# A transformer block on one core: first norm with tokens on partitions, and the first stage's vector work regrouped

## The chip, the core and the metric

The kernel runs on one core of a Trainium2 chip. The metric is the device time of one execution in microseconds (us), lower is better. The core has five engines that run their own instruction streams: TensorE (PE, matrix products), VectorE (DVE), ScalarE (ACT), GpSimd (POOL) and SyncE (SP, which here issues every transfer). An engine takes its instructions in order and waits on semaphores for the others.

## The reference

One block with 256 tokens and 1024 features, all in float32. `c` makes six vectors of 1024 (shift, scale and gate of two halves), the normed input is scaled and shifted by them, one wide projection gives seven parts, and attention, a gating unit and a feed-forward follow:

```python
mod = silu(c) @ w_ada + b_ada                      # shift1, scale1, gate1, shift2, scale2, gate2
h = rmsnorm(x, g_mix) * (1 + scale1) + shift1
q, k, v, u, vs, ga, gb = split(h @ w_in)           # 512,512,512,512,512,1024,1024 columns
y_attn = causal_attention(q, k, v) @ w_proj_attn   # 8 heads of 64
y_sgu = spatial_gating(gelu(u), gelu(vs)) @ w_proj_sgu
x = x + gate1 * ((sigmoid(ga) * y_attn + sigmoid(gb) * y_sgu) @ w_out)
h = rmsnorm(x, g_ffn) * (1 + scale2) + shift2
x = x + gate2 * (square(relu(h @ w_ff1)) @ w_ff2)  # 4096 wide
return rmsnorm(x, g_final)
```

`rmsnorm` divides each token by the root of the mean of its squares (plus 1e-6).

## The kernel before

**Products.** A float32 product is made of three products in a faster 32-bit format. Every operand is split into a high part (ACT's cast `whi`, `hh`) and the rest (DVE's subtraction `wlo`, `hl`), and PE adds high·high, high·low and low·high in one accumulator. So each weight chunk of 128 x 2048 costs ACT a cast, DVE a subtraction and PE 48 or 36 products, and it arrives by a transfer of 1 MB into one of five `raw` buffers. Accumulators are banks of a pool of eight (`bank()`).

**Head.** SP loads a table of columns (`cols_sb`), x turned (`xT`, features on partitions) into `x_sb`, and the first chunks. ACT squares x, DVE adds the four squares, PE sums them over the partitions (`sums`), ACT and POOL make one over the root (`rstd`), and PE spreads it over all partitions (`spread`). POOL then multiplies seven of the eight feature tiles of x by it (`xn`, line 298), DVE the first. PE also runs small idle products (`spin`).

**First stage (lines 250 to 330).** A loop of eight turns, one for each tile `kt` of 128 features. A turn has two chunks: one of `w_ada` (columns of scale1 and shift1) and one of `w_in` (columns for q, k, v and vs). DVE makes two dot products of the ada chunk with silu(c) (`junk`, each with a sum `acc`), from them the columns `acol` and `bcol`; ACT makes `hh` = xn · acol + bcol, DVE the same in full precision (`hf`) and the difference `hl`; ACT and DVE split the `w_in` chunk; PE then runs 24 products of 256 columns and 12 of 512. In this stage the order of PE, DVE and ACT is that of the code (`InOrder`, pinned). I call the moment when PE starts the first product of turn k S(k).

**Middle and rest.** From `high(0)` on the order is not pinned: a scheduler lays out what each engine issues. In ten turns PE runs u, ga and gb (`wide(n)`) from streamed chunks while ACT, DVE and PE also do attention (pairs of heads: scores, exponentials, norm, transposes, products with v) and the gating unit. Then come the projections, `w_out`, the feed-forward in 16 units and the last norm. `x_sb` is read again as the residual at `w_out`.

Of the kernel before, what the change touches and what calls it, by code (L numbers as in the profile page):

```python
# [34 lines left out]
class InOrder:  # L35
    """An engine whose instructions are issued in the order in which they are traced."""
# [11 lines left out]
def block_kernel(ctx, tc, xT, cols, wsguT, bsgu, w_a1, w_1, w_a, w_m, w_f, out):  # L48
# [138 lines left out]

    # the middle's weight chunks, and the adaLN chunks that are used beside them
# [62 lines left out]
    hh = act.tile([P, KT, S], F32R, name="hh", tag="b1")  # L251
    hl = act.tile([P, KT, S], F32R, name="hl", tag="b2")
    rb1 = wk.tile([P, S], F32, name="rb1", tag="sqa", bufs=1)
    xn = act.tile([P, KT, S + 2], F32, name="xn", tag="b3")
    wsg = const.tile([P, 8, P], F32, name="wsg", tag="c4")
    bsg = const.tile([P, NP, P], F32, name="bsg")
    for kt in range(KT):
        if kt + 2 < KT:
            ada[kt + 2] = load(w_a1[kt + 2], 2 if kt + 2 == KT - 1 else 1)
            wraw[kt + 2] = load(w_1[kt + 2], 4 if kt + 2 == KT - 1 else 2)  # L260
        raw, w_raw = ada.pop(kt), wraw.pop(kt)
        np_ = 4 if kt in (0, KT - 1) else 2
        wh = his.tile([P, 2048], F32R, name="whi", tag="whi")
        wl = los.tile([P, 2048], F32R, name="wlo", tag="wlo")
        hf = wk.tile([P, S], F32, name="hf", tag="hf", bufs=2)
        wp = [slice(2048 // np_ * i, 2048 // np_ * (i + 1)) for i in range(np_)]

        def w_hi(i):
            ACT.copy(out=wh[:, wp[i]], in_=w_raw[:, wp[i]])

        def w_lo(i):
            DVE.tensor_tensor(out=wl[:, wp[i]], in0=w_raw[:, wp[i]], in1=wh[:, wp[i]].bitcast(F32), op=ALU.subtract)

        def cols_ab():
            column(da, SCALE1, kt)
            column(db, SHIFT1, kt)

        def h_hi():
            a, b = acol[:, 0, kt:kt + 1], bcol[:, 0, kt:kt + 1]
            ACT.activation(out=hh[:, kt], in_=xn[:, kt, 0:S], func=AF.Identity, scale=a, bias=b)  # L280
            DVE.tensor_scalar(out=hf, in0=xn[:, kt, 0:S], scalar1=a, scalar2=b, op0=ALU.mult, op1=ALU.add)

        def h_lo():
            DVE.tensor_tensor(out=hl[:, kt], in0=hf, in1=hh[:, kt].bitcast(F32), op=ALU.subtract)

        da, db = dot(raw, 0), dot(raw, 1)
        if kt == 0:
            for i in range(3):
                w_hi(i)
            cols_ab()  # L290
            rp = spread(rs1)
            spin(4)
            DVE.tensor_tensor(out=xn[:, 0, 0:S], in0=x_sb[:, 0], in1=rp[:, 0:S], op=ALU.mult)
            h_hi()
# [9 lines left out]
            qk_ps = [bank() for _ in range(4)]
            vv_ps = [[bank() for _ in range(2)] for _ in range(2)]
        else:
            w_hi(0)
            cols_ab()
            h_hi()
            w_lo(0)  # L310
            w_hi(1)
            h_lo()
            for i in range(1, np_):
                w_lo(i)
                if i + 1 < np_:
                    w_hi(i + 1)
        f, l = kt == 0, kt == KT - 1
        for ft in range(8):
            o = qk_ps[ft // 2][:, S * (ft % 2):S * (ft % 2) + S]
            w = slice(P * ft, P * ft + P)  # L320
            mm3(o, wh[:, w], wl[:, w], hh[:, kt], hl[:, kt], f and ft % 2 == 0, l,
                skip_group_check=ft % 2 == 1)
        for n in range(2):
            w = slice(1024 + 512 * n, 1536 + 512 * n)
            for t in range(2):
                tk = slice(P * t, P * t + P)
                o = vv_ps[n][t]
                PE.matmul(out=o, lhsT=hh[:, kt, tk], rhs=wh[:, w], start=f, stop=False)
                PE.matmul(out=o, lhsT=hl[:, kt, tk], rhs=wh[:, w], start=False, stop=False)
                PE.matmul(out=o, lhsT=hh[:, kt, tk], rhs=wl[:, w], start=False, stop=l)  # L330
# [134 lines left out]
    A0, S0, TD, OD = 1, 5, 2, 3  # when attention and the gating unit start; lags of transposes and products  # L465
    for n in range(10):
# [7 lines left out]
        if n == 0:  # L474
# [240 lines left out]
def _ko(w, cols):  # L715
    """[K, N] -> chunks [N/cols][128][K/128 * cols] with k in (ko, p)."""
# [42 lines left out]
```

## Time and profile before

| | us |
|---|---|
| median of 3 runs (lowest, highest) | 376.79 (376.47, 377.02) |
| span of the profiled execution, first to last instruction | 374.84 |
| around the span, to that median | 1.95 |
| PE busy | 358.4 (96%) |
| DVE busy | 266.4 (71%) |
| ACT busy | 206.0 (55%) |
| POOL busy | 15.4 (4%) |

The profiled execution's own time is known by its span; what lies around the span is taken from the median. Busy time is an average over stages, and PE's 96% hides where it waits. PE's waits as the profile lists them are 3.3 and 3.1 us in the head, 2.4 us for `hl`, 1.2 us for `hh` and 0.5 us for the root.

### The profile page before, as it was taken

Reading aid. Unit: us, or ns where it says so; the run is one execution under the profiler, and the core shown is the slowest. Engines: PE = TensorE matmul, PEld = TensorE weight load, DVE = VectorE, ACT = ScalarE, POOL = GpSimd, SP = SyncE. Lnnn points to the kernel's source line nnn. Section 1 sums busy time; section 2 is a strip of 40 time slices with the busy share of each in tenths; the row PEclk is TensorE's granted clock in tenths of the full one; section 3 lists DMA queues with packets and bytes.
Section 4 is the critical chain, followed back from the end, with each engine's and each line's share of the span. In section 5 each row is a group of like instructions: output and inputs, shape, how many; then the busy total and the mean of one; then the engine's idle time right before and its main releaser. Section 6 shows DMA issues by size and latency. Waiting matters only on the chain.

```text
span 374.8 us, 6928 instructions
## 1 busy us (share of the span) xinstructions
PE 358.4 (96%) x2884; PEld 346.5 (92%) x2884; DVE 266.4 (71%) x420; ACT 206.0 (55%) x283; POOL 15.4 (4%) x21
## 2 busy tenths in 40 slices
PE   4779999999999999999999999999999999999993
PEld 3469989999899999999999999999999999999993
DVE  2899997687989986899856755766656545546442
ACT  4424346999894374356566544655445645446242
POOL 1460000010000000000000000000000000000001
PEclk9999999999999999999999999999999999999997
DMA  7999999987789995467755494764856554500003
GB/s 246 410 348 346 346 348 398 320 321 259 269 309 357 353 396 226 152 232 282 251 210 189 150 334 147 299 231 150 299 202 257 217 201 147 215 1 2 2 0 112
DMA packets 16126, 89.34 MB, mean 238 GB/s; under 512 B 1888, under 2 KB 2400, under 8 KB 7136
## 3 DMA queue, kind: packets, MB, share of 16 engines
q1 hardware_dynamic: 16096, 88.92, 64.9%
q8 instruction: 22, 0.36, 0.4%
q14 instruction: 8, 0.07, 0.0%
HBM read 87.86 MB, written 1.05 MB: 237 GB/s over the span
## 4 chain that ended last, share of the span: by engine, by line
PE 92%; issue 3%; DVE 3%; POOL 1%; POOLq 0%; DVEq 0%; ACT 0%
PE bank L44 92%; DVE junk L44 1%; DVE wlo L44 1%; POOL rs L120 0%; DVE hl L44 0%; DVE ys L44 0%; POOLq L755 0%; DVEq L755 0%; DVE acol L44 0%; DVE xn L44 0%; POOL maskf L103 0%; DVE maskf L44 0%; DVE idle L44 0%; ACT ms L44 0%; DVE ones L44 0%
## 5 line engine op out<-in xcount | busy, mean ns | idle before, releaser
L44 ACT CAST whi<-raw 128x2048 fp32r<-128x2048 f32 (+2 forms) x74 | 112.6, 1537 | 79.3 <-PE bank L44 77.7
L44 DVE TENSOR_TENSOR wlo<-raw,whi 128x2048 fp32r<-128x2048 f32 (+2 forms) x74 | 135.8, 1842 | 9.1 <-ACT whi L44 7.9
L44 PE MATMUL bank<-zh,whi 128*128 128x258 f32 x256 | 72.5, 283 | 0.0
L44 PE MATMUL bank<-zh,wlo 128*128 128x258 f32 x256 | 72.3, 282 | 0.0
L44 PE MATMUL bank<-zl,whi 128*128 128x258 f32 x256 | 72.2, 282 | 0.0
L44 PE MATMUL bank<-fl,whi 128*128 128x256 f32 x256 | 72.0, 281 | 0.0
L44 PE MATMUL bank<-fh,wlo 128*128 128x256 f32 x256 | 71.9, 281 | 0.0
L44 PE MATMUL bank<-fh,whi 128*128 128x256 f32 x256 | 71.9, 281 | 0.0
L44 PE MATMUL bank<-hl,whi 128*128 128x256 f32 x224 | 63.5, 283 | 2.4 <-DVE hl L44 2.4
L44 PE MATMUL bank<-hh,whi 128*128 128x256 f32 x224 | 64.5, 288 | 1.2 <-ACT hh L44 1.2
L44 PE MATMUL bank<-hh,wlo 128*128 128x256 f32 x224 | 63.3, 282 | 0.0
L44 DVE SCALAR_TENSOR_TENSOR junk<-raw,csb 128x1024 bf16<-128x1024 f32 x48 | 58.4, 1239 | 0.0
L44 PEld LDWEIGHTS bank<-fh,whi 128*128 128x128 f32 x256 | 49.1, 192 | 0.0
L44 PEld LDWEIGHTS bank<-zl,whi 128*128 128x128 f32 x256 | 48.4, 189 | 0.0
L44 PEld LDWEIGHTS bank<-zh,whi 128*128 128x128 f32 x256 | 48.3, 189 | 0.0
L44 PEld LDWEIGHTS bank<-zh,wlo 128*128 128x128 f32 x256 | 48.3, 189 | 0.0
L44 PEld LDWEIGHTS bank<-fh,wlo 128*128 128x128 f32 x256 | 48.1, 188 | 0.0
L44 PEld LDWEIGHTS bank<-fl,whi 128*128 128x128 f32 x256 | 48.0, 188 | 0.0
L44 PEld LDWEIGHTS bank<-hh,whi 128*128 128x128 f32 x224 | 42.9, 192 | 3.2 <-ACT hh L44 2.0
L44 PEld LDWEIGHTS bank<-hl,whi 128*128 128x128 f32 x224 | 42.7, 191 | 3.3 <-DVE hl L44 2.9
L44 PEld LDWEIGHTS bank<-hh,wlo 128*128 128x128 f32 x224 | 42.8, 191 | 0.0
L44 DVE TENSOR_TENSOR fl<-r,fh 128x512 fp32r<-128x512 f32 x16 | 11.1, 694 | 30.2 <-PE bank L44 28.9
(132 smaller groups left out, 488.7 us busy)
## 6 DMA issues: line engine op xcount, KB each, us to landing
raw<-in_w_f SPq DMA_DIRECT2D x32, 1024.0 KB, 4.8
raw<-in_w_a SPq DMA_DIRECT2D x22, 1024.0 KB, 5.8
raw<-in_w_m SPq DMA_DIRECT2D x16, 1024.0 KB, 6.5
raw<-in_w SPq DMA_DIRECT2D x12, 512.0 KB, 6.6
raw<-in_w_a SPq DMA_DIRECT2D x4, 512.0 KB, 6.8
raw<-in_w SPq DMA_DIRECT2D x8, 256.0 KB, 7.2
x_sb<-in_xT SPq DMA_DIRECT2D x2, 512.0 KB, 5.2
raw<-in_w_m SPq DMA_DIRECT2D x4, 256.0 KB, 6.8
```

Of the source, the lines that this page charges most:

```text
L44: return lambda *a, **k: pin(op(*a, **k))
```

## The change

- x is loaded with tokens on partitions (`xt`, one half per transfer). ACT's square sums each token by itself (an added column holds the 1e-6), POOL makes one over the root per half, DVE scales the first half and ACT the second, and PE turns both with 16 transposes into four banks (`xps`). `xn` is copied from there by ACT (`keep`). POOL multiplies nothing; one POOL power is issued early on constants.
- `x_sb` is loaded from `xT` later, in the middle's sixth turn, for the residual alone. The gating unit's tables are loaded two turns later than before.
- In the first stage's turns after the first, ACT makes `acol`, `bcol` and `hf` too. DVE keeps the dots, `wlo` and `hl`.
- PE's products of a turn go pass by pass (all high·high, then high·low, then low·high) and not column tile by column tile. Their number is the same.
- Idle products: 8 and 6 in place of 4 and 4. The turned banks are allocated, and those of q, k, v and vs too, ahead of the loop.

```diff
-    for i in range(2):
-        nc.sync.dma_start(out=x_sb[:, 4 * i:4 * i + 4], in_=xT[:, 4 * i:4 * i + 4])
+    for t in range(2):
+        nc.sync.dma_start(out=xt[:, t, 0:D], in_=x[t])
+        DVE.memset(xt[:, t, D:D + 1], (EPS * D) ** 0.5)
...
+    rs1 = const.tile([P, 2], F32, name="rs1")
+    nc.gpsimd.tensor_tensor(out=rs1, in0=ones[:, 0:2], in1=nhalf, op=ALU.pow)
...
-    for i in range(4):
-        ACT.activation(out=sqs[i], in_=x_sb[:, 2 * i:2 * i + 2], func=AF.Square)
-        if i:
-            DVE.tensor_tensor(out=sqs[0], in0=sqs[0], in1=sqs[i], op=ALU.add)
...
-    spin(4)
-    rs1 = rstd(ss, D)
+    for t in range(2):
+        sq = act.tile([P, D + 1], F32, name="sq", tag=("b1", "b2")[t])
+        ACT.activation(out=sq, in_=xt[:, t], func=AF.Square, scale=D ** -0.5, accum_out=ms1[:, t:t + 1])
+        nc.gpsimd.tensor_tensor(out=rs1[:, t:t + 1], in0=ms1[:, t:t + 1], in1=nhalf[:, 0:1], op=ALU.pow)
+    DVE.tensor_scalar(out=xt[:, 0, 0:D], in0=xt[:, 0, 0:D], scalar1=rs1[:, 0:1], scalar2=None, op0=ALU.mult)
+    for w in (slice(0, P), slice(P, D)):
+        ACT.activation(out=xt[:, 1, w], in_=xt[:, 1, w], func=AF.Copy, scale=rs1[:, 1:2])
+    xps = [bank() for _ in range(4)]
+    for t in range(2):
+        for kt in range(KT):
+            at = S * (kt % 2) + P * t
+            PE.transpose(out=xps[kt // 2][:, at:at + P], in_=xt[:, t, P * kt:P * kt + P], identity=ident)
+    spin(6)
...
+            if n == 0:
+                ACT.activation(out=bcol[:, n, at], in_=acc, func=AF.Identity, bias=b)
+            else:
+                DVE.tensor_tensor(out=bcol[:, n, at], in0=acc, in1=b, op=ALU.add)
...
-            for i in range(1, KT):
-                nc.gpsimd.tensor_tensor(out=xn[:, i, 0:S], in0=x_sb[:, i], in1=rb1, op=ALU.mult)
...
+        column(db, SHIFT1, kt)
+        ACT.activation(out=hh[:, kt], in_=xk, func=AF.Identity, scale=a, bias=b)
+        if f:
+            DVE.tensor_scalar(out=hf, in0=xk, scalar1=a, scalar2=b, op0=ALU.mult, op1=ALU.add)
+        else:
+            ACT.activation(out=hf, in_=xk, func=AF.Identity, scale=a, bias=b)
             w_lo(0)
...
+        for fts in (range(0, 4), range(4, 8)) if np_ == 4 else (range(0, 8),):
+            for p, (w, h) in enumerate(((wh, hh), (wh, hl), (wl, hh))):
+                for ft in fts:
...
+        if n == 5:
+            nc.sync.dma_start(out=x_sb, in_=xT)
-        if n == 0:
+        if n == 2:
             nc.sync.dma_start(out=wsg, in_=wsguT)
```

Three places of the order in which the engines now issue. The first is DVE in one turn of the first stage, from the two dots of a turn to the dots of the next; before:

```order
L44 SCALAR_TENSOR_TENSOR junk,acc<-raw,csb 128x1024 x2
L44 SCALAR_TENSOR_TENSOR acol<-acc,cols_sb,pre 128x1
L44 TENSOR_TENSOR bcol<-acc,cols_sb 128x1
L44 TENSOR_SCALAR hf<-xn,acol,bcol 128x256
L44 TENSOR_TENSOR wlo<-raw,whi 128x1024
L44 TENSOR_TENSOR hl<-hf,hh 128x256
L44 TENSOR_TENSOR wlo<-raw,whi 128x1024
L44 SCALAR_TENSOR_TENSOR junk,acc<-raw,csb 128x1024 x2
```

The same turn on DVE now:

```order
L44 SCALAR_TENSOR_TENSOR junk,acc<-raw,csb 128x1024 x2
L44 TENSOR_TENSOR wlo<-raw,whi 128x1024
L44 TENSOR_TENSOR hl<-hf,hh 128x256
L44 TENSOR_TENSOR wlo<-raw,whi 128x1024
L44 SCALAR_TENSOR_TENSOR junk,acc<-raw,csb 128x1024 x2
```

Three instructions have left DVE's turn; the second `wlo` still stands ahead of the next turn's dots. The second place is ACT in a turn of the first stage, from the cast of a chunk's first half on; before:

```order
L44 CAST whi<-raw 128x1024
L44 ACTIVATE hh<-xn,bcol,acol 128x256
L44 CAST whi<-raw 128x1024 x2
L44 ACTIVATE hh<-xn,bcol,acol 128x256
L44 CAST whi<-raw 128x1024 x2
```

The same on ACT now (the pair of casts is the second half of this turn's chunk and the first half of the next one's):

```order
L44 CAST whi<-raw 128x1024
L44 ACTIVATE acol<-acc,pre,cols_sb 128x1
L44 ACTIVATE bcol<-acc,cols_sb 128x1
L44 ACTIVATE hh<-xn,bcol,acol 128x256
L44 ACTIVATE hf<-xn,bcol,acol 128x256
L44 CAST whi<-raw 128x1024 x2
```

`acol`, `bcol` and `hf` have come to ACT, and the cast of the second half stands behind them. The third place is ACT in the middle, where the second pair of heads is normed (`pr<-pr,rc`), the first pair's transposes are copied (`pt`) and the third pair's exponentials follow (`pr,sm<-bank,mx`, four pieces); before:

```order
L44 ACTIVATE pr<-pr,rc 128x128
L44 COPY pt<-bank 128x384
L44 CAST whi<-raw 128x2048
L44 COPY pt<-bank 128x384
L44 ACTIVATE pr,sm<-bank,mx 128x256
L44 ACTIVATE pr,sm<-bank,mx 128x128
L44 ACTIVATE pr,sm<-bank,mx 128x256
```

The same place now:

```order
L44 ACTIVATE ga_sb<-bank 128x2x256
L44 COPY pt<-bank 128x384 x2
L44 ACTIVATE pr<-pr,rc 128x256
L44 ACTIVATE pr<-pr,rc 128x128
L44 ACTIVATE pr<-pr,rc 128x256
L44 ACTIVATE pr<-pr,rc 128x128
L44 ACTIVATE pr,sm<-bank,mx 128x256
L44 CAST whi<-raw 128x2048
L44 ACTIVATE pr,sm<-bank,mx 128x128
```

A chunk's cast now stands between the first and the second piece of the third pair's exponentials. PE's own order from the first attention product on is the same as before.

## Rows read from the trace of the kernel before

**Rows 1.** Chain that ended last: start us, us, what.

```profile
26.07 341.85 PE bank L44 x2807
```

**Rows 2.** Timeline of PE, first stage: start us, us, operation, wait before.

```profile
24.55 0.38 PE L44 MATMUL bank<-hh,whi 128*128 128x256 f32 x1 [1.23 <-ACT hh L44]
...
28.02 0.41 PE L44 MATMUL bank<-hl,whi 128*128 128x256 f32 x1
28.23 0.41 PE L44 MATMUL bank<-hh,wlo 128*128 128x256 f32 x1
...
33.20 0.28 PE L44 MATMUL bank<-hh,whi 128*128 128x256 f32 x1
...
61.34 0.28 PE L44 MATMUL bank<-hh,whi 128*128 128x256 f32 x1
```

**Rows 3.** Busy by stretch: PE, PEld, DVE, ACT, POOL, granted clock, DMA share, GB/s.

```profile
28.00:29.00 1.00, 1.00 (x7) 1.00 (x6) 1.00 (x3) 0.00 (x0) 0.00 (x0) 0.50 0.83 209
```

**Rows 4.** Timeline of all engines, head and first turn.

```profile
6.10 2.44 ACT L44 ACTIVATE sq<-x_sb 128x512 f32<-128x512 f32 x4 [3.37 <-DMA x_sb<-in_xT]
...
10.96 1.87 PE L44 MATMUL bank<-idle 128*128 128x512 bf16 x4
...
11.48 1.75 POOL L120 TENSOR_TENSOR rs<-ms,nhalf 128x2 f32<-128x2 f32 x1 [9.39 <-ACT ms L44]
...
15.94 8.46 POOL L298 TENSOR_TENSOR xn<-x_sb,rb 128x256 f32<-128x256 f32 x7 [2.70 <-ACT rb L44]
...
19.70 1.76 DVE L44 SCALAR_TENSOR_TENSOR junk<-raw,csb 128x1024 bf16<-128x1024 f32 x1
```

**Rows 5.** Transfers: timeline of SP, and time to landing of the transfers issued from 6.0, 9.9.

```profile
6.09 0.33 SPq L66 DMA_DIRECT2D raw<-in_w_a  x1
7.38 1.61 SPq L66 DMA_DIRECT2D raw<-in_w  x2
9.94 0.33 SPq L66 DMA_DIRECT2D raw<-in_w_a  x1
...
raw<-in_w_a SPq DMA_DIRECT2D x1, 1024.0 KB, 10.0
...
raw<-in_w_a SPq DMA_DIRECT2D x1, 1024.0 KB, 11.2
```

**Rows 6.** Timeline of DVE and ACT in one turn of the first stage.

```profile
27.07 1.21 DVE L44 SCALAR_TENSOR_TENSOR junk<-raw,csb 128x1024 bf16<-128x1024 f32 x1
...
28.21 0.08 DVE L44 DVE_READ_ACCUMULATOR junk<-raw,csb 128x1 f32 x1
...
29.50 0.15 DVE L44 TENSOR_TENSOR bcol<-acc,cols_sb 128x1 f32<-128x1 f32 x1
29.74 0.60 ACT L44 ACTIVATE hh<-xn,bcol,acol 128x256 fp32r<-128x256 f32 x1 [3.36 <-DVE bcol L44]
...
30.24 1.98 ACT L44 CAST whi<-raw 128x1024 fp32r<-128x1024 f32 x2
...
31.55 1.22 DVE L44 TENSOR_TENSOR wlo<-raw,whi 128x1024 fp32r<-128x1024 f32 x1
32.69 1.22 DVE L44 SCALAR_TENSOR_TENSOR junk<-raw,csb 128x1024 bf16<-128x1024 f32 x1
```

**Rows 7.** Groups by form: busy us, mean ns, idle before and its releaser.

```profile
L44 ACT ACTIVATE ms<-bank,eps 128x2 f32<-128x2 f32 x3 | 0.8, 259 | 2.5 <-PE bank L44 2.5
...
L496 POOL TENSOR_TENSOR vrs<-vms,nhalf 128x2 f32<-128x2 f32 x1 | 0.7, 698 | 46.3 <-DVE vms L44 46.3
```

**Rows 8.** Middle: timeline of ACT and PE, and ACT's casts of the streamed chunks (group).

```profile
62.24 0.60 ACT L44 ACTIVATE qT<-bank 128x512 f32<-128x512 f32 x1 [1.73 <-PE bank L44]
...
92.65 0.40 ACT L44 ACTIVATE pr<-bank,mx 128x128 f32<-128x128 f32 x1
...
96.49 0.39 PE L44 MATMUL bank<-hh,whi 128*128 128x256 f32 x1
...
L44 ACT CAST whi<-raw 128x2048 fp32r<-128x2048 f32 x48 | 91.7, 1913 | 77.7 <-PE bank L44 77.7
```

More of the change, by code (lines that the diff above doesn't have):

```diff
@@ L47, in block_kernel @@
 @with_exitstack
-def block_kernel(ctx, tc, xT, cols, wsguT, bsgu, w_a1, w_1, w_a, w_m, w_f, out):
+def block_kernel(ctx, tc, x, xT, cols, wsguT, bsgu, w_a1, w_1, w_a, w_m, w_f, out):
     nc = tc.nc
@@ L76, in block_kernel @@
     nc.sync.dma_start(out=cols_sb, in_=cols)
+    xt = act.tile([P, 2, D + 1], F32, name="xt", tag="b4")
+    for t in range(2):
+        nc.sync.dma_start(out=xt[:, t, 0:D], in_=x[t])
+        DVE.memset(xt[:, t, D:D + 1], (EPS * D) ** 0.5)
     x_sb = act.tile([P, KT, S], F32, name="x_sb")
-    for i in range(2):
-        nc.sync.dma_start(out=x_sb[:, 4 * i:4 * i + 4], in_=xT[:, 4 * i:4 * i + 4])
     ada = {0: load(w_a1[0], 2)}
@@ L83, in block_kernel @@
     wraw[1] = load(w_1[1], 2)
+    ada[2] = load(w_a1[2])
     idle = wk.tile([P, 12 * P], BF16, name="idle", tag="pt")[:, 0:512]
@@ L141, in block_kernel @@
                   start=kt % 4 == 0, stop=True, skip_group_check=kt % 4 > 0)
-    ss = bank()
-    sqs = [act.tile([P, 2, S], F32, name="sq", tag=t) for t in ("q1", "q2", "o1", "o2")]
-    for i in range(4):
-        ACT.activation(out=sqs[i], in_=x_sb[:, 2 * i:2 * i + 2], func=AF.Square)
-        if i:
-            DVE.tensor_tensor(out=sqs[0], in0=sqs[0], in1=sqs[i], op=ALU.add)
-    DVE.tensor_tensor(out=sqs[0][:, 0], in0=sqs[0][:, 0], in1=sqs[0][:, 1], op=ALU.add)
-    sums(ss, sqs[0][:, 0], True, True)
-    for i in range(2):
-        ACT.copy(out=csb[:, 512 * i:512 * i + 512], in_=cps[i])
-    spin(4)
-    rs1 = rstd(ss, D)
+    spin(8)
+    for i in range(2):
+        DVE.tensor_copy(out=csb[:, 512 * i:512 * i + 512], in_=cps[i])
+    ms1 = const.tile([P, 2], F32, name="ms1")
+    for t in range(2):
[11 more added lines that the diff above has]
+    spin(6)
     identb = const.tile([P, P], BF16, name="identb")
@@ L178, in column @@
         if part in (SCALE1, SCALE2):
-            g = (G_MIX, G_FFN)[n]
-            DVE.scalar_tensor_tensor(out=acol[:, n, at], in0=acc, scalar=cols_sb[:, g + kt:g + kt + 1],
-                                     in1=pre[:, n, at], op0=ALU.mult, op1=ALU.add)
+            known = pre[:, n, at]
+            g = cols_sb[:, (G_MIX, G_FFN)[n] + kt:(G_MIX, G_FFN)[n] + kt + 1]
+            if n == 0:
+                ACT.activation(out=acol[:, n, at], in_=acc, func=AF.Identity, scale=g, bias=known)
+            else:
+                DVE.scalar_tensor_tensor(out=acol[:, n, at], in0=acc, scalar=g, in1=known, op0=ALU.mult, op1=ALU.add)
         elif part in (SHIFT1, SHIFT2):
-            DVE.tensor_tensor(out=bcol[:, n, at], in0=acc, in1=b, op=ALU.add)
+            if n == 0:
+                ACT.activation(out=bcol[:, n, at], in_=acc, func=AF.Identity, bias=b)
+            else:
+                DVE.tensor_tensor(out=bcol[:, n, at], in0=acc, in1=b, op=ALU.add)
         else:
@@ L252, in block_kernel @@
     hl = act.tile([P, KT, S], F32R, name="hl", tag="b2")
-    rb1 = wk.tile([P, S], F32, name="rb1", tag="sqa", bufs=1)
-    xn = act.tile([P, KT, S + 2], F32, name="xn", tag="b3")
+    xn = act.tile([P, KT, S], F32, name="xn", tag="b3")
     wsg = const.tile([P, 8, P], F32, name="wsg", tag="c4")
     bsg = const.tile([P, NP, P], F32, name="bsg")
+    qk_ps = [bank() for _ in range(4)]
+    vv_ps = [[bank() for _ in range(2)] for _ in range(2)]
     for kt in range(KT):
+        f, l = kt == 0, kt == KT - 1
         if kt + 2 < KT:
-            ada[kt + 2] = load(w_a1[kt + 2], 2 if kt + 2 == KT - 1 else 1)
+            if kt:
+                ada[kt + 2] = load(w_a1[kt + 2], 2 if kt + 2 == KT - 1 else 1)
             wraw[kt + 2] = load(w_1[kt + 2], 4 if kt + 2 == KT - 1 else 2)
         raw, w_raw = ada.pop(kt), wraw.pop(kt)
-        np_ = 4 if kt in (0, KT - 1) else 2
+        np_ = 4 if f or l else 2
         wh = his.tile([P, 2048], F32R, name="whi", tag="whi")
@@ L266, in block_kernel @@
         wp = [slice(2048 // np_ * i, 2048 // np_ * (i + 1)) for i in range(np_)]
+        xk = xps[0][:, 0:S] if f else xn[:, kt]
+        a, b = acol[:, 0, kt:kt + 1], bcol[:, 0, kt:kt + 1]
         def w_hi(i):
@@ L272, in w_lo, with keep @@
             DVE.tensor_tensor(out=wl[:, wp[i]], in0=w_raw[:, wp[i]], in1=wh[:, wp[i]].bitcast(F32), op=ALU.subtract)
-        def cols_ab():
+        def keep(i):
+            ACT.copy(out=xn[:, 2 * i:2 * i + 2], in_=xps[i].rearrange("p (i t) -> p i t", i=2))
+        da = dot(raw, 0)
+        if f:
             column(da, SCALE1, kt)
[L276 to L294, printed above, removed]
-            w_lo(0)
-            ACT.copy(out=rb1, in_=rp[:, 0:S])
-            for i in range(1, KT):
-                nc.gpsimd.tensor_tensor(out=xn[:, i, 0:S], in0=x_sb[:, i], in1=rb1, op=ALU.mult)
-            w_lo(1)
-            h_lo()
+        db = dot(raw, 1)
@@ new lines, in block_kernel @@
+        w_hi(0)
+        if not f:
+            column(da, SCALE1, kt)
+        column(db, SHIFT1, kt)
+        ACT.activation(out=hh[:, kt], in_=xk, func=AF.Identity, scale=a, bias=b)
+        if f:
+            DVE.tensor_scalar(out=hf, in0=xk, scalar1=a, scalar2=b, op0=ALU.mult, op1=ALU.add)
+        else:
+            ACT.activation(out=hf, in_=xk, func=AF.Identity, scale=a, bias=b)
+            w_lo(0)
+        w_hi(1)
+        DVE.tensor_tensor(out=hl[:, kt], in0=hf, in1=hh[:, kt].bitcast(F32), op=ALU.subtract)
@@ L301, in block_kernel @@
+        if f:
+            w_lo(0)
+        w_lo(1)
+        if np_ == 4:
+            w_hi(2)
             w_lo(2)
+            if f:
+                keep(0)
+                keep(1)
             w_hi(3)
             w_lo(3)
[L304 to L322, printed above, removed]
-        for n in range(2):
[L324 to L330, printed above, removed]
+            if f:
+                keep(2)
+                keep(3)
@@ new lines, in block_kernel @@
+        for fts in (range(0, 4), range(4, 8)) if np_ == 4 else (range(0, 8),):
+            for p, (w, h) in enumerate(((wh, hh), (wh, hl), (wl, hh))):
+                for ft in fts:
+                    PE.matmul(out=qk_ps[ft // 2][:, S * (ft % 2):S * (ft % 2) + S], lhsT=w[:, P * ft:P * ft + P],
+                              rhs=h[:, kt], start=f and p == 0 and ft % 2 == 0, stop=l and p == 2,
+                              skip_group_check=ft % 2 == 1)
+        for n in range(2):
+            c = slice(1024 + 512 * n, 1536 + 512 * n)
+            for p, (h, w) in enumerate(((hh, wh), (hl, wh), (hh, wl))):
+                for t in range(2):
+                    PE.matmul(out=vv_ps[n][t], lhsT=h[:, kt, P * t:P * t + P], rhs=w[:, c],
+                              start=f and p == 0, stop=l and p == 2)
@@ L734 @@
     ins = {
+        "x": a["x"][0].reshape(2, P, D),
         "xT": a["x"][0].T.reshape(KT, P, S).transpose(1, 0, 2),
```

## The prediction, made before the changed kernel was run

> **What bounds the kernel now.** I read the chain of waits first. From 26.07 us on it is PE alone, 341.85 us in one piece [rows 1]; PE then never waits. So only what comes before, or a new wait of PE, can move the end. The 374.84 us span is 1.95 us below the 376.79 us median, and I add terms to the span and carry them to the median unchanged.
>
> Next I read PE's timeline in the first stage. Turn 2 starts at 33.20 and turn 7 at 61.34 [rows 2], so a turn in which PE waits for nothing takes 28.14/5 = 5.63 us, and phase two starts at 61.34 + 5.63 = 66.97. Eight such turns are 45.0 us, so PE's first stage carries 66.97 - 45.0 = 22 us of head, waits and slow clock. Turn 1 starts at 24.55 after a wait for `hh`, waits again for `hl` until 26.07 [rows 1, 2], and then runs at the lower clock: at 28.02 to 28.23 a product follows the last one after 0.21 us, with a granted clock of 0.50 [rows 2, 3], which is 1.2 GHz. At full speed a turn is 5.63/48 = 0.117 us per 256 columns (24 products of 256 and 12 of 512 are 48 units).
>
> Last I read the timeline of the other engines. ACT starts on x at 6.10; POOL's root takes 1.75 us and runs until 13.23; POOL's seven multiplications take 8.46 us from 15.94 on, and a dot of DVE that runs beside them takes 1.76 us [rows 4] where a later one takes 1.21 [rows 6]. The trace shows the pair slower together; it doesn't say what they share.
>
> **The change, part by part.** *Head.* The second half of x has landed at 7.38, since SP's next transfer, which waits for it, is issued then [rows 5]; the head's order on SP is the same now. ACT's square of 1025 columns is like the 1024-column cast, 1.0 us [rows 6], plus about 0.1 for the sum: 8.5. POOL's power takes 0.70 as in its second use [rows 7] or 1.75 as in its first [rows 4]; there is one earlier on constants, so I take 0.70: 9.25. ACT scales the second half in two pieces, 1.3 us: 10.6. The last needed transposes end near 10.9. Beside this DVE copies csb, scales the first half by 9.2 (0.6 to 1.1 us for 1024 columns, neither hurts), and makes two dots, 1.14 + 1.22 us [rows 6], until 11.8. ACT's `bcol` and `hh` follow: PE's first product at about 12.9. Before, POOL's root alone ended at 13.23, and the spread, `xn` and `hh` came behind it.
>
> *Turn 0 to turn 1.* DVE needs `hf`, `hl` and four `wlo` of turn 0, until 16.0. The ada chunk of turn 1 was issued at 6.09 and lands 10.0 later, at 16.1 [rows 5]. So turn 1's dots start at 16.2 (19.70 before, [rows 4]). From a dot's start to PE's first product it is 1.14 (dot) + 1.22 (dot, sum read) + 0.09 (handover, 29.65 to 29.74, [rows 6]) + 0.26 (`bcol` on ACT, like the 128x2 `ms` [rows 7]) + 0.04 + 0.60 (`hh`) + 0.05 = 3.40. S(1) = 19.6 us, against 24.55 and a real start at 26.07. Turn 0's 5.63 us from 12.9 end before that, with `keep`'s copies beside them, so PE waits about 1 us here.
>
> *Turns 1 to 7.* On DVE 0.25 us of columns and 0.33 of `hf` leave a turn that was exactly full (dots 27.07 to 32.69 is 5.62, [rows 6]). But the order now closes a loop over two engines: two dots on DVE, then `bcol`, `hh`, `hf` and the cast of the second half on ACT, then the second `wlo` on DVE, and only behind it the next dots. Behind the waiting `bcol` stand ACT's `hh`, `hf` and both casts; behind the waiting `wlo` the next turn's dots, and PE waits for all of these. With the rows: 1.14 + 1.22 + 0.09 + 0.26 + 0.04 + 0.50 (`hh` to the next, 29.74 to 30.24) + 0.50 (`hf`, alike) + 1.03 (cast) + 0.04 + 1.14 (`wlo` to the next dot, 31.55 to 32.69) = 5.96 us [rows 6, 7]. That is 0.33 us more than PE's turn. `bcol` on ACT between two DVE operations isn't in the trace, so I bound the turn: 5.63, PE's own pace, if something overlaps that the order doesn't show, and 6.4 if the three handovers and `bcol` cost twice as much (0.43 more). I take 5.96, the plain sum of the nearest rows. S(7) = 19.6 + 6 x 5.96 = 55.4, which is 6.0 us ahead of 61.34.
>
> *Transfers.* A turn needs 2 MB per 5.96 us. Turn 2's ada chunk is issued at 9.94 and lands 11.2 later, at 21.1 [rows 5], and its dots come at 22.2; later chunks are released earlier than before and have more room. Cost nothing, 1 us of cover at the tightest.
>
> *PE's order.* Pass by pass has the same 36 products per turn, each with its own weights as before: nothing. Its gain is cover for `hl` and `wlo`, since 8 products (0.94 us) now run on `hh` alone; `hl` comes some 0.8 us after `hh` (0.50 of `hf`, 0.33 of `hl`), so the second wait, that until 26.07, goes.
>
> *Middle.* `x_sb` adds 1 MB, 2.8 us at the first stage's 2 MB per turn. All idle time of ACT ahead of the 48 big casts was ended by PE, none by a transfer [rows 8], so these chunks land early and hide it; I take nothing, and 2.8 us at most. What does change is ACT's lead. Before, turn 2's `hh` was done at 30.34, 2.9 us ahead of S(2) = 33.20 [rows 2, 6], and turn 7's as much, since DVE and PE kept the same pace. Now it is just in time. ACT's copies of q start at S(7) + 3.9 (1.0 for `hh` and `hf` from S(7) - 0.6 on, then seven 512-column casts of 0.5, half a 1024-column one) where they started at S(7) + 0.9 (62.24, [rows 8]). The tightest place behind it is the fifth `wide`, which PE reached at 96.49, S(7) + 35.2 [rows 8], and whose bank is freed by the second exponential of the third pair. That ended at 93.05, 30.8 us after the copies began, of which 1.5 was three small casts that now stand ahead of the copies. The new order puts a 1.9 us cast between the pieces [rows 8] and leaves about 0.5 more waiting on the gating unit's root (0.70 on POOL [rows 7], part of it covered). So it ends at S(7) + 3.9 + 29.3 + 1.9 + 0.5 = S(7) + 35.6: PE waits 0.4 us. Bounds: 0, and 3 if ACT is later by the whole lead that it lost.
>
> **Sum.** -6.0 + 0.4 = -5.6 us: 374.84 - 5.6 = 369.2 span, 376.79 - 5.6 = **371.2 us**.
>
> **Rivals.** *A. The loop hides, PE's pace sets the stage.* S(7) = 19.6 + 6 x 5.63 = 53.4, 7.9 us ahead, and ACT has a lead again: 368.9. For it: PE alone was the bound from turn 2 on. Against: the printed order, which has no other work to fill the loop.
>
> *B. The clock is low in turn 0.* Before turn 0 PE now runs idle products, 16 transposes and six idle products, with gaps. Before, the four idle products of 512 columns at 10.96 took 1.87 us [rows 4], 0.47 each where full speed would be 0.23, and after the waits that end at 26.07 PE ran at 0.50 [rows 3]. If all of turn 0 runs at 1.2 GHz it takes 11.3 us; S(1) = 24.2, PE then sets the pace, S(7) = 58.0: 3.3 us ahead, ACT has its lead again, 373.5. If it rises within the first half of turn 0, the loop hides it all. The Trainium skill, "TensorE: Matmul & The Clock Gate", section "Part 4: PE-mode transpose", speaks for this rival: it says that transposes don't count as PE work for the clock. By that rule the 16 transposes buy no speed for turn 0; no row here shows it either way.
>
> *C. ACT stalls the middle.* The 3 us of lost lead come back as waits of PE, 2.6 more than in the sum: 373.8. For it: the sum above has no slack at one place. Against: other places have 1 us or more.
>
> *D. Slower: the loop over ACT is dearer.* One mechanism at one place, the handovers DVE to ACT to DVE in turns 1 to 6. From (61.34 - 19.6)/6 = 6.96 us a turn it eats the whole head gain, 1.0 us above my sum. At 7.2 a turn S(7) = 62.8, and with the middle's 0.4: 376.79 + 1.5 + 0.4 = 378.7. For it: `bcol` on ACT is unseen and four waits are in each turn. Against: the handover that is seen takes 0.09 [rows 6].
>
> *E. The change does nothing,* because the first chunks land when they land: 376.8. For it: the early chunks take 10 us to land [rows 5]. Against: turn 1's dots started 3.6 us after their chunk had landed (19.70 against 16.1, [rows 4, 5]).
>
> **Chances.** Forecast (370.2 to 372.3) 0.58, A 0.12, B 0.11, C 0.09, D 0.06, E 0.04. The forecast's own range is 370.2 to 372.3; with A below and B and C above, 368.6 to 374.6 holds 8 in 10 with room. A measurement here can tell 0.2%, 0.75 us, from no change: faster is the forecast, A, B and C, 0.90; same is E and the edge of D, 0.05; slower 0.05.
>
> **What would show it.** Right: PE's first product near 12.9, turn 1 near 19.6, turns of 5.9 to 6.0 us with a short wait for `hh` at the start of each (0.3 us), `bcol` on ACT near 0.26, no dot above 1.25 us, no granted clock of 0.5 between turn 1 and turn 2, PE in one piece from S(7) on but for less than 1 us in the middle. Wrong: turns of 5.63 without waits (A), a product pace of 0.21 in turn 0 and no wait for turn 1 (B), waits for ACT's `pr` or `whi` past turn 7 (C), turns of 7 us (D), or dots that wait for a transfer (E).

## The result, and the profile after

| | before | after |
|---|---|---|
| median, us (lowest, highest, runs) | 376.63 (374.85, 377.02, 4) | 370.50 (370.36, 371.28, 4) |
| span of the profiled execution | 374.84 | 368.3 |
| S(1), S(7), first attention scores | 24.55, 61.34, 72.71 | 18.48, 54.13, 66.13 |

The ratio is 0.9865 (95% interval 0.9832 to 0.9898), so the change saves 5.1 us (3.8 to 6.3); the medians differ by 6.1 and the spans by 6.5. The forecast was 371.2, a saving of 5.6. A second set of runs gave 370.86 and 0.9862 (0.9836 to 0.9888).

Timeline of the kernel after, all engines, head and turn 0 (start us, us, operation, idle time before it and what ended it); it answers to [rows 4, 5]:

```profile
6.09 1.06 ACT L44 ACTIVATE sq<-xt 128x1025 f32<-128x1025 f32 x1 [0.15 <-DMA xt<-in_x]
...
7.32 1.08 POOL L156 TENSOR_TENSOR rs<-ms,nhalf 128x1 f32<-128x1 f32 x1 [0.68 <-ACT sq L44]
7.62 0.74 DVE L44 TENSOR_SCALAR xt<-xt,rs 128x1024 f32<-128x1024 f32 x1
...
8.43 1.22 DVE L44 SCALAR_TENSOR_TENSOR junk<-raw,csb 128x1024 bf16<-128x1024 f32 x1
...
11.77 0.54 DVE L44 TENSOR_SCALAR hf<-bank,acol,bcol 128x256 f32<-128x256 f32 x1 [0.96 <-ACT hh L44]
...
12.39 0.83 PE L44 MATMUL bank<-hh,whi 128*128 128x256 f32 x4
...
12.68 2.49 DVE L44 TENSOR_TENSOR wlo<-raw,whi 128x512 fp32r<-128x512 f32 x4
...
15.09 1.22 DVE L44 SCALAR_TENSOR_TENSOR junk<-raw,csb 128x1024 bf16<-128x1024 f32 x1
...
15.98 1.05 ACT L44 CAST whi<-raw 128x1024 fp32r<-128x1024 f32 x1 [0.76 <-DMA raw<-in_w]
...
17.50 0.29 ACT L44 ACTIVATE bcol<-acc,cols_sb 128x1 f32<-128x1 f32 x1 [0.17 <-DVE junk L44]
...
18.48 1.21 PE L44 MATMUL bank<-hh,whi 128*128 128x256 f32 x8
```

The chain of the head runs over DVE now: dots from 8.43, a wait of 0.96 us for ACT's `hh`, then `hf`, `hl`, four `wlo`, and turn 1's dots at 15.09. From there to PE's product are 3.39 us. Timeline of DVE and ACT in one turn, which answers to [rows 6]:

```profile
26.98 1.22 DVE L44 SCALAR_TENSOR_TENSOR junk<-raw,csb 128x1024 bf16<-128x1024 f32 x1
...
28.12 1.22 DVE L44 SCALAR_TENSOR_TENSOR junk<-raw,csb 128x1024 bf16<-128x1024 f32 x1
...
29.38 0.30 ACT L44 ACTIVATE bcol<-acc,cols_sb 128x1 f32<-128x1 f32 x1 [0.57 <-DVE junk L44]
29.71 0.60 ACT L44 ACTIVATE hh<-xn,bcol,acol 128x256 fp32r<-128x256 f32 x1
30.22 0.59 ACT L44 ACTIVATE hf<-xn,bcol,acol 128x256 f32<-128x256 f32 x1
30.71 1.03 ACT L44 CAST whi<-raw 128x1024 fp32r<-128x1024 f32 x1
30.84 0.43 DVE L44 TENSOR_TENSOR hl<-hf,hh 128x256 fp32r<-128x256 f32 x1 [0.35 <-ACT hf L44]
31.78 1.23 DVE L44 TENSOR_TENSOR wlo<-raw,whi 128x1024 fp32r<-128x1024 f32 x1 [0.51 <-ACT whi L44]
...
32.92 1.22 DVE L44 SCALAR_TENSOR_TENSOR junk<-raw,csb 128x1024 bf16<-128x1024 f32 x1
```

Dots to dots take 32.92 - 26.98 = 5.94 us, and the loop can be read off: two dots on DVE, `bcol`, `hh`, `hf` and a cast on ACT, then the `wlo` that waited 0.51. Groups of DVE from 18 to 55 us (busy us, mean ns, idle time before and what ended it) show what it idles for, 6.1 us in all:

```profile
L44 DVE TENSOR_TENSOR wlo<-raw,whi 128x1024 fp32r<-128x1024 f32 x12 | 14.7, 1222 | 3.1 <-ACT whi L44 3.1
L44 DVE SCALAR_TENSOR_TENSOR junk<-raw,csb 128x1024 bf16<-128x1024 f32 x12 | 14.2, 1218 | 0.0
L44 DVE TENSOR_TENSOR hl<-hf,hh 128x256 fp32r<-128x256 f32 x7 | 3.0, 425 | 3.0 <-ACT hf L44 3.0
```

Timeline of PE and ACT from turn 7 to the fifth `wide`, for [rows 2, 8], and the chain's last long piece, for [rows 1]:

```profile
54.13 0.73 PE L44 MATMUL bank<-hh,whi 128*128 128x256 f32 x4
55.08 0.75 PE L44 MATMUL bank<-hl,whi 128*128 128x256 f32 x4 [0.22 <-DVE hl L44]
...
60.34 0.28 PE L44 MATMUL bank<-hh,whi 128*128 128x256 f32 x1
...
87.35 1.89 ACT L44 CAST whi<-raw 128x2048 fp32r<-128x2048 f32 x1
89.14 0.36 ACT L44 ACTIVATE pr<-bank,mx 128x128 f32<-128x128 f32 x1
...
90.04 0.39 PE L44 MATMUL bank<-hh,whi 128*128 128x256 f32 x1
```

```profile
55.08 301.39 PE bank L44 x2544
```

Turn 7 takes 60.34 - 54.13 = 6.21 us, 0.58 more than PE's 5.63: only four products of 0.12 us cover the wait for `hl`. The lead over the kernel before is 7.2 us at S(7), 6.6 at the first scores and 6.5 at the end of the profiled executions.

### The profile page after: what moved, and what is told of

It reads as the page before. It is cut to its first block, busy times and chain, and to the rows that moved or that the text cites. A ratio compares the mean times of both kernels' runs of the same rounds, so it can differ in the third digit from the quotient of the medians.

```text
span 368.3 us, 6942 instructions
## 1 busy us (share of the span) xinstructions
PE 358.6 (97%) x2898; PEld 345.6 (94%) x2898; DVE 259.3 (70%) x397; ACT 216.4 (59%) x308; POOL 9.5 (3%) x16
## 4 chain that ended last, share of the span: by engine, by line
PE 83%; DMA 9%; DVE 4%; issue 1%; ACT 1%; POOLq 0%; POOL 0%; DVEq 0%; SPq 0%
PE bank L44 83%; DMA raw<-in_w 5%; DVE junk L44 3%; DMA raw<-in_w_a 2%; DMA raw<-in_w_m 1%; DMA cols_sb<-in_cols 0%; DVE wlo L44 0%; ACT hf L44 0%; ACT whi L44 0%; DVE x_sb L44 0%; POOLq L772 0%; DVE ys L44 0%; POOL sq L699 0%; DVE sq L44 0%; DVEq L772 0%
## 5 line engine op out<-in xcount | busy, mean ns | idle before, releaser
L44 DVE TENSOR_TENSOR wlo<-raw,whi 128x2048 fp32r<-128x2048 f32 (+2 forms) x74 | 134.4, 1826 | 15.2 <-ACT whi L44 14.8
L44 DVE SCALAR_TENSOR_TENSOR junk<-raw,csb 128x1024 bf16<-128x1024 f32 x48 | 57.3, 1217 | 0.0
L44 PE MATMUL bank<-hh,whi 128*128 128x256 f32 x224 | 55.9, 289 | 0.3
L44 PE MATMUL bank<-hl,whi 128*128 128x256 f32 x224 | 54.4, 282 | 0.2 <-DVE hl L44 0.2
L44 PE MATMUL bank<-hh,wlo 128*128 128x256 f32 x224 | 54.4, 282 | 0.0
L44 PEld LDWEIGHTS bank<-fh,whi 128*128 128x128 f32 x256 | 48.1, 188 | 0.0
L44 PEld LDWEIGHTS bank<-hh,whi 128*128 128x128 f32 x224 | 38.5, 188 | 4.4 <-ACT hh L44 3.4
L44 PEld LDWEIGHTS bank<-hl,whi 128*128 128x128 f32 x224 | 38.4, 188 | 0.5 <-DVE hl L44 0.4
L44 PEld LDWEIGHTS bank<-hh,wlo 128*128 128x128 f32 x224 | 38.4, 188 | 0.0
```

The lines of the kernel that those rows point to most:

```text
L44: return lambda *a, **k: pin(op(*a, **k))
```

## The experiments

Every kernel below is the kernel after with one edit, unless it says otherwise; none leaves work out. Ratios are to the kernel before on the same chip.

| | median us | ratio (95%) | S(1) | S(7) | first scores |
|---|---|---|---|---|---|
| casts first | 369.33 | 0.9821 (0.9800-0.9843) | 19.86 | 53.87 | 65.32 |
| `hf` twice | 375.49 | 0.9991 (0.9972-1.001) | 19.57 | 59.02 | 71.85 |
| columns on DVE | 368.49 | 0.9801 (0.9778-0.9823) | 18.39 | 52.53 | 63.95 |
| tile by tile | 372.28 | 0.9903 (0.9882-0.9923) | 19.76 | 55.61 | 67.31 |
| no idle products | 370.44 | 0.9858 (0.9821-0.9896) | 18.60 | 54.26 | 66.33 |
| `x_sb` in head | 373.24 | 0.9930 (0.9902-0.9958) | 21.37 | 57.04 | 69.10 |
| GpSimd beside | 373.10 | 0.9920 (0.9896-0.9944) | 22.39 | 57.33 | 69.33 |
| head alone | 369.36 | 0.9809 (0.9791-0.9827) | 19.07 | 53.58 | 65.00 |
| before, by passes | 374.76 | 0.9958 (0.9941-0.9976) | 24.59 | 59.03 | 70.40 |
| turns 0 and 1 | 368.13 | 0.9785 (0.9768-0.9802) | 18.76 | 53.19 | 64.60 |

**The kernel after once more,** with no edit.

> The changed kernel unchanged, as the measure for the other runs of this chip. In two of the kernels run so far the first dots waited for the first ada chunk until 9.1 us and in three they did not (8.4 or earlier). If the landing of the head's transfers varies from execution to execution, the time is 370.0 to 371.5 and the first dot anywhere from 8.3 to 9.2; if it belongs to those kernels, the first dot is at 8.4 again and S(1) at 18.5.

370.86 us (370.42 to 371.33), first dot at 8.51, S(1) 18.74: the measure for the others holds. PE, which waited for nothing in the middle of the first profile, waited here at the fifth `wide`:

```profile
90.71 0.39 PE L44 MATMUL bank<-hh,whi 128*128 128x256 f32 x1 [0.25 <-ACT pr L44]
```

**Is the loop what sets a turn? Casts first.**

```diff
         if not f:
+            w_hi(1)
             column(da, SCALE1, kt)
...
-        w_hi(1)
+        if f:
+            w_hi(1)
```

> The changed kernel, but in turns 1 to 7 ACT's cast of the second half (quarter in turn 7) stands ahead of acol, bcol, hh and hf, so that the next dots no longer wait for work that waits for this turn's dots. Theory, the loop over DVE and ACT sets the 5.94 us of a turn: turns fall to PE's own 5.63 to 5.70 us, S(7) is near 52.5 (54.13 in the changed kernel), and the time is about 1.6 us lower, 368.9. Rival, the transfers set the pace (DMA share 1.0 until 40 us, ACT's cast of the first half waits 0.8 to 1.7 us for them): turns stay at 5.9 or more, the casts' waits for the DMA hold acol and bcol up, time 370.5 or higher.

Turns fell to 5.67 us ((53.87 - 19.86)/6): the loop set them. But S(1) came 1.4 us later. Timeline of ACT and PE:

```profile
17.65 1.05 ACT L44 CAST whi<-raw 128x1024 fp32r<-128x1024 f32 x1 [0.23 <-DMA raw<-in_w]
...
19.86 1.22 PE L44 MATMUL bank<-hh,whi 128*128 128x256 f32 x8 [1.53 <-ACT hh L44]
```

The second half of turn 1's chunk lands at 17.6, and the columns now stand behind its cast. So the rival held for turn 1 alone. The gain over the kernel after is 0.4% by the ratios, whose intervals overlap (0.9821 and 0.9865): what this run shows of the loop is the length of its turns, and not the time.

**The loop made longer: `hf` twice.**

```diff
             ACT.activation(out=hf, in_=xk, func=AF.Identity, scale=a, bias=b)
+            ACT.activation(out=hf, in_=xk, func=AF.Identity, scale=a, bias=b)
```

> The changed kernel with hf computed twice on ACT in turns 1 to 7, 0.50 us more inside the loop. Theory, the loop sets the turn: turns of 6.44 us, S(7) near 57.1 (54.13), time 3.0 to 3.5 us higher, near 373.8. Rival, the transfers set the pace and the loop only follows them: at most 1 us more, 371.5.

The rival fell: turns take 6.58 us ((59.02 - 19.57)/6), 0.64 more, for a second `hf` of about 0.6 (the pair took 1.22, one 0.59). The time rose by more than forecast, 1.3% by the ratios: 3.8 us in six turns, 1.1 at S(1), where the first dot waited for its chunk until 9.12 in this execution, 0.7 later, and 0.8 in turn 7, where `hl` is later too.

**The regrouping undone: columns on DVE.**

```diff
-            if n == 0:
+            if n == 0 and kt == 0:
                 ACT.activation(out=bcol[:, n, at], in_=acc, func=AF.Identity, bias=b)
...
-            ACT.activation(out=hf, in_=xk, func=AF.Identity, scale=a, bias=b)
+            DVE.tensor_scalar(out=hf, in0=xk, scalar1=a, scalar2=b, op0=ALU.mult, op1=ALU.add)
             w_lo(0)
```

> The changed kernel with acol, bcol and hf of turns 1 to 7 back on DVE as in the kernel before; head, products pass by pass, GpSimd without products stay. Theory, the new head brings the whole gain and the regrouping costs the loop: a turn of DVE is 5.62 us as in the kernel before, PE keeps that pace, S(7) near 52.2 (54.13), time about 1.8 us lower, 368.7. Rival, the regrouping pays, DVE being the tighter engine: turns of 6 us or more, time 371 or higher.

As expected: 0.64% or 2.4 us faster than the kernel after (0.9801 against 0.9865; the intervals do not overlap). Groups of DVE, 18 to 53 us, and PE's turns:

```profile
L44 DVE TENSOR_TENSOR wlo<-raw,whi 128x1024 fp32r<-128x1024 f32 x12 | 14.6, 1218 | 0.0
L44 DVE TENSOR_TENSOR hl<-hf,hh 128x256 fp32r<-128x256 f32 x7 | 2.9, 419 | 0.0
```

```profile
24.40 1.11 PE L44 MATMUL bank<-hh,whi 128*128 128x256 f32 x8
...
30.03 1.11 PE L44 MATMUL bank<-hh,whi 128*128 128x256 f32 x8
```

DVE does more and idles 0.3 us in all (ahead of `hf`) in place of 6.1, and PE's turns are 5.63 from turn 2 on. The regrouping took 0.6 us of work off DVE and gave it waits in return.

**The order of the products: tile by tile.** The old loop over column tiles stands in place of the passes.

```diff
-        for fts in (range(0, 4), range(4, 8)) if np_ == 4 else (range(0, 8),):
-            for p, (w, h) in enumerate(((wh, hh), (wh, hl), (wl, hh))):
+        for ft in range(8):
+            o = qk_ps[ft // 2][:, S * (ft % 2):S * (ft % 2) + S]
+            w = slice(P * ft, P * ft + P)
+            mm3(o, wh[:, w], wl[:, w], hh[:, kt], hl[:, kt], f and ft % 2 == 0, l,
```

> The changed kernel with PE's products of a turn tile by tile as before. Theory, the order only covers hl: PE waits for hl in each turn (hl is 0.8 us behind hh, one product of 0.12 covers it), but since the loop of 5.94 leaves PE 0.3 us a turn, PE slips 0.4 us behind once and then keeps the pace; with turn 7, whose hl it must wait for anyway, the time is 0.2 to 0.5 us higher, near 370.9. Rival, the order is a main part of the gain (PE waited 2.4 us for hl in the kernel before): 0.7 us lost in each of seven turns, 4 to 5 us more, 375.

Between the two: 0.4% slower than the kernel after by the ratios, whose intervals overlap. PE did slip (turn 1 took 6.11 us) and then kept 5.95 us a turn. A part was unforeseen: PE waited 0.92 us for `pr` in the middle. Another execution of the same kernel (span 369.8) shows where, in the timelines of ACT and PE:

> The changed kernel with products tile by tile once more, for one look. If the late first dot (9.19 in place of 8.4) belongs to the execution, it is at 8.3 to 8.5 here, S(7) near 54.8, and the wait for pr in the middle (0.92) is shorter or gone; if it belongs to the kernel, all three are there again.

```profile
79.45 1.19 ACT L44 ACTIVATE pr<-pr,rc 128x256 f32<-128x256 f32 x3
80.54 1.89 ACT L44 CAST whi<-raw 128x2048 fp32r<-128x2048 f32 x1
82.33 0.40 ACT L44 ACTIVATE pr<-pr,rc 128x128 f32<-128x128 f32 x1
82.78 0.55 PE L44 MATMUL bank<-ident,pr 128*128 128x128 f32 x3 [0.90 <-ACT pr L44]
```

The first dot was early here (8.48 against 9.19), so the landing belongs to the execution. The wait for `pr` was there again: with the edit the scheduler had put a cast of 1.89 us between the last two norms, ahead of PE's transposes. So the order of products itself is worth less than the 1.4 us that the ratios show.

**The clock: no idle products.** Both `spin(8)` and `spin(6)` are taken out.

> The changed kernel without its 14 idle products of 512 columns. Theory, the idle products keep the clock up and the 16 transposes alone do not: the first products run at 1.2 GHz (0.21 us each in place of 0.12), turn 0 ends up to 5 us later, S(1) at 20 to 23 in place of 18.5, time 1.5 to 3 us higher, near 372.5. Rival, real work keeps the clock up: first product 0.6 us earlier (11.8), S(1) the same, since DVE sets it, time 370.5.

The rival held: no change. Timeline of PE:

```profile
8.37 3.65 PE L44 MATMUL bank<-ident,xt 128*128 128x128 f32 x16 [1.45 <-DVE xt L44]
11.89 0.74 PE L44 MATMUL bank<-hh,whi 128*128 128x256 f32 x4
...
14.11 0.64 PE L44 MATMUL bank<-hh,whi 128*128 128x256 f32 x4
14.59 0.64 PE L44 MATMUL bank<-hl,whi 128*128 128x256 f32 x4
```

From 14.11 on four products take 0.48 us, 0.12 each, which is the pace at 2.4 GHz, at a granted clock of 1.00. Since its pause before 8.37 PE had done only the transposes and three passes of turn 0, the later of these at 0.15 a product. The transposes had taken 3.65 us, where the same 16 took 1.91 in the kernel after, and here too the granted clock was 1.00.

**The transfers: `x_sb` in the head.**

```diff
     x_sb = act.tile([P, KT, S], F32, name="x_sb")
+    nc.sync.dma_start(out=x_sb, in_=xT)
...
-        if n == 5:
-            nc.sync.dma_start(out=x_sb, in_=xT)
```

> The changed kernel with the 1 MB of x_sb loaded right behind x, ahead of the first weights, and not in the middle. Theory, the head's transfers have under 1 us of cover (the dots of turn 1 start 0.5 us after their chunk has landed) and run at 415 GB/s, so 1 MB is 2.5 us and S(1) comes 2 to 2.5 us later; time near 372.8. Rival, the transfers have room: at most 0.5 us, 371.0.

As the theory had it, 0.65% slower: S(1) is 2.9 us later, since DVE's first dot waits for its chunk.

```profile
11.22 1.22 DVE L44 SCALAR_TENSOR_TENSOR junk<-raw,csb 128x1024 bf16<-128x1024 f32 x1 [2.54 <-DMA raw<-in_w_a]
```

**GpSimd beside DVE.**

```diff
+    for i in range(7):
+        nc.gpsimd.tensor_tensor(out=x_sb[:, i], in0=xt[:, 1, 0:S], in1=csb[:, 0:S], op=ALU.mult)
     spin(6)
```

> The changed kernel with seven GpSimd products of 128 x 256 beside turn 0, as in the kernel before, their results overwritten by the later load of x_sb. Theory, GpSimd and VectorE slow each other when both run (a dot took 1.76 us beside them, 1.21 without): DVE's 7 us of turn 0 take 30 to 45% longer, S(1) near 20.5 to 21.5, time 2 to 3 us higher, near 373. Rival, the slower dot of the kernel before had another cause: dots stay at 1.22, time 370.5.

The theory held, with 2.1 us (0.55%). Groups of DVE while GpSimd runs, then GpSimd's timeline, then PE's stretch from 17 to 18 us (busy of PE, PEld, DVE, ACT, POOL, granted clock, DMA share, GB/s):

```profile
L44 DVE SCALAR_TENSOR_TENSOR junk<-raw,csb 128x1024 bf16<-128x1024 f32 x2 | 3.4, 1738 | 0.6 <-DMA raw<-in_w_a 0.6
L44 DVE TENSOR_TENSOR hl<-hf,hh 128x256 fp32r<-128x256 f32 x1 | 0.7, 682 | 0.0
L44 DVE TENSOR_SCALAR hf<-bank,acol,bcol 128x256 f32<-128x256 f32 x1 | 0.5, 544 | 1.0 <-ACT hh L44 1.0
```

```profile
9.18 7.42 POOL L166 TENSOR_TENSOR x_sb<-xt,csb 128x256 f32<-128x256 f32 x7 [1.45 <-ACT xt L44]
```

```profile
17.00:18.00 1.00, 1.00 (x6) 1.00 (x6) 1.00 (x3) 0.38 (x2) 0.00 (x0) 0.50 1.07 446
```

A dot took 1.74 us in place of 1.22, `hl` 0.68 in place of 0.42; `hf`, whose one tensor comes from a bank of PSUM here, kept its 0.54. The Trainium skill, "GPSIMD Engine Reference", "1. Specifications", says that GpSimd shares its SBUF interfaces with VectorE and contends with instructions that have two SBUF inputs; these rows agree. PE then waited three times in turn 0, its granted clock fell to 0.50 (1.2 GHz), and S(1) moved by 3.9, more than expected. By S(7) 3.2 of it were left (this execution took 373.97 us, the median is 373.10).

**The head alone.** Columns on DVE and products tile by tile, that is the kernel before with the new head and without GpSimd's products; both edits are shown above.

> The kernel before with the new head alone: acol, bcol and hf of turns 1 to 7 on DVE, products tile by tile. Theory, the head brings all of the gain and more: S(1) 18.4 as with the columns on DVE, PE waits once more for hl in turn 1 (0.75 us more than with products pass by pass) and then keeps 5.63 us a turn behind it, since DVE has its lead again; time 369.2. Rival, the order of the products is worth a wait for hl in each turn: 4 us more, 372.5 or higher.

369.36, as expected: the head brings the whole gain and 2 us more. It differs from columns on DVE by less than the runs can tell (0.9809 and 0.9801).

**The kernel before with products by passes** (the new loop in the old kernel).

> The kernel before with PE's products pass by pass and nothing else changed. Theory, the order only covers hl and only where PE waits for it, in turns 0 and 1: the first eight products of turn 1 run while hl is made, 0.8 to 1.2 us less, time near 375.6. Rival, the order is worth little beside the slow clock that follows the waits: less than 0.4 us, 376.4.

0.42% or 1.6 us faster, more than expected. Timeline of PE in turn 1, the kernel before and then this kernel, which starts turn 2 at 30.90:

```profile
26.07 0.45 PE L44 MATMUL bank<-hl,whi 128*128 128x256 f32 x1 [1.14 <-DVE hl L44]
```

```profile
26.11 1.21 PE L44 MATMUL bank<-hl,whi 128*128 128x256 f32 x8 [0.31 <-DVE hl L44]
...
30.90 1.10 PE L44 MATMUL bank<-hh,whi 128*128 128x256 f32 x8
```

Stretch from 27 to 28 us, this kernel:

```profile
27.00:28.00 1.00, 1.00 (x11) 1.00 (x10) 1.00 (x2) 0.00 (x0) 0.00 (x0) 1.00 0.67 262
```

The kernel before stood at 0.50 there, as in [rows 3]. In the profiled executions, one of each kernel, S(2) came 2.3 us earlier: 0.8 is the shorter wait, the rest the clock, which here stayed at full speed (1.00). That the shorter wait is what kept it there is likely, but not shown: over whole executions of the kernel before the mean granted clock ran from 0.982 to 0.996, so the slow stretch may differ from one execution to the next.

**Turns 0 and 1,** on top of columns on DVE.

```diff
-    spin(6)
...
+        if f:
+            w_lo(0)
         DVE.tensor_scalar(out=hf, in0=xk, scalar1=a, scalar2=b, op0=ALU.mult, op1=ALU.add)
-            w_lo(0)
+        if kt > 1:
+            w_lo(0)
...
-        for fts in (range(0, 4), range(4, 8)) if np_ == 4 else (range(0, 8),):
+        for fts in (range(0, 4), range(4, 8)) if l else (range(0, 8),):
```

> The kernel with the columns on DVE, and three edits in turns 0 and 1: DVE's first wlo of turn 0 stands ahead of hf, where DVE waited 0.96 us; the six idle products are gone and turn 0's passes go over all eight tiles; in turn 1 hl stands ahead of the first wlo. Theory, DVE's chain through turn 0 sets S(1): dots of turn 1 start 0.5 us earlier, S(1) at 17.9 in place of 18.4, no wait for hl in turn 1 (0.27), time 0.6 to 0.8 us lower, 367.8. Rival, the transfers hold it: the ada chunk of turn 1 lands at 14.6 and the first half of w_in at 16.0, gain 0.2 us or less, 368.4.

368.13 is the lowest of all medians, but its interval overlaps that of columns on DVE, and S(1) is 18.76, not 17.9. Timeline of DVE:

```profile
14.83 0.69 DVE L44 TENSOR_TENSOR wlo<-raw,whi 128x512 fp32r<-128x512 f32 x1 [0.31 <-ACT whi L44]
15.44 1.22 DVE L44 SCALAR_TENSOR_TENSOR junk<-raw,csb 128x1024 bf16<-128x1024 f32 x1
```

DVE lost its new lead to ACT's casts and to a first dot at 8.94 that waited 0.38 for its chunk. The theory failed; these edits can't be told from nothing.

## Why the prediction was right

**Head: right in kind, 1.1 us too long.** S(1) was put at 19.6 and came at 18.48. Two landings were taken too late: x's second half at 7.38, by the next transfer's issue, where ACT had it at 6.09, and turn 1's chunk at 16.1, where it was issued at 5.13 and landed 9.5 later. DVE's dots of turn 0, put at 9.4 to 11.8, ran from 8.43 to 10.8, and so its part of the turn, put at 16.0, was done at 15.1. The step from dot to product, 3.40, was 3.39. Turn 0 ran at full speed. POOL's second power was put at 0.70 and took 1.08, which cost nothing, since ACT's scaling behind it was done at 9.8 (forecast 10.6).

**Turns: right.** 5.96 forecast, 5.94 measured. That the DVE-ACT loop sets them was only argued then; columns on DVE, casts first and `hf` twice show it. `bcol` on ACT, put at 0.26, took 0.30 and `acol` 0.39. The Trainium skill, "ScalarE: Activation LUTs", "What ACT_TABLE_LOAD costs", gives about 280 ns with a bias pointer, and 93 more for each further pointer: the rows agree.

**PE's order: the step that failed.** That the second wait for `hl` goes held for turn 1. But in turn 7 the passes go over four tiles, 0.48 us of cover, and PE has `hl` 0.95 us after its start: 0.47 of the 0.58 lost there, counted at nothing.

**Transfers: right that nothing was lost, but tighter than said.** The forecast looked at the dots' chunks alone. In turn 1 ACT's first cast waited 0.76 us for its half chunk, and `bcol`, behind it on ACT, then waited only 0.17 us for DVE's dot: a landing 0.2 us later would have moved S(1). Moving the second cast ahead cost 1.4 us there (casts first), 1 MB more in the head 2.9.

**Middle: 0.4 forecast, 0 measured here.** The third pair's second exponential ended at 89.50, S(7) + 35.4 (forecast 35.6). PE reached the place at S(7) + 35.9 and not 35.2, since turn 7 had held it up, so it found the bank free. In the second profile of the kernel after it waited 0.25 us there.

**Sum.** To S(7) the gain was 7.2 and not 6.0; turn 7 took 0.6 back; the middle took nothing: 6.5 and not 5.6 by the spans (5.1 by the ratio). The larger head and the missed wait partly offset each other, so the number came closer than its terms, and a part of that is luck.

**Rivals.** A's price (368.9) is near that of a kernel without the loop: columns on DVE has 368.49. B (clock) fell: turn 0 ran at full speed, even without idle products. The rule of the Trainium skill on transposes ("TensorE: Matmul & The Clock Gate", "Part 4: PE-mode transpose"), by which turn 0 would have been slow, did not decide here: without idle products the transposes were slow, and the products behind them reached 0.12 us. Whether the transposes or the 16 products ahead of the pause did that is open. C's place is real, with 0 to 0.25 us. D fell with turns of 5.94 us and not 7, E with S(1) 6.1 us earlier.

The forecast had the loop's price, 0.33 us a turn, but left out that the parts pull against each other: head alone 0.9809, with passes 0.9801, with the regrouping as well 0.9865. Columns on DVE beats both kernels. Of the head's own parts, GpSimd's products are worth 2.1 us and the idle products nothing that could be told; the turned load, the early power and the banks were run together only.

## What to carry to other kernels

When work moves off a full engine, write down the order of both engines and look for a cycle: the second engine's work may stand between two pieces of the first one's turn, and the waits can cost more than the work moved. Split a change into its parts before keeping all of it: here one part earned 7.2 us (head alone, by its ratio) and another gave 2.4 back. And when a pass over tiles covers a latency, check the turn where the pass is shorter.

## What the runs showed of the hardware

- DVE instructions with two SBUF inputs took 1.4 to 1.6 times as long beside GpSimd's products (1.74 for 1.22, 0.68 for 0.42); one whose only tensor came from PSUM did not (0.54).
- In no idle products the first eight transposes took 1.97 us, where all 16 of the kernel after took 1.91, both at a granted clock of 1.00: the granted clock does not show every slow stretch of PE.
- The landing of the head's first ada chunk varied between executions of one kernel by 0.7 us or more: the first dot waited for it until 9.19 in one execution of tile by tile, and started at 8.48 without a wait in the other.
- Of GpSimd's powers on 128x1 one took 0.55 us and the next 1.08 in the same execution. The longer one ran beside DVE's scaling of `xt` and ended 0.04 us after it (8.40 and 8.36); in columns on DVE it started earlier, at 7.16, and took 0.55. The power of 1.75 us in the kernel before started beside DVE's dots, which ended at 12.68, and ended 0.55 us after them. No run tests this by itself. But being the first power, as the forecast read [rows 4], does not explain the 1.75 us: the first of the kernel after, on constants, took 0.70.
